# A hybrid decoder block on one core: the final norm's small operations over four token tiles at once, and the A products of two heads issued by turns

## The chip, the cores and the metric

The kernel runs on one core of a Trainium2 chip, as one program. The metric is the device time of one execution in microseconds, taken as the median of a few executions. The core's engines are TensorE (PE in the profile, with its weight loads as PEld), VectorE (DVE), ScalarE (ACT), GpSimd (POOL) and SyncE (SP), which issues the DMAs of this kernel. Each engine takes its own instructions in the order in which they stand in the program.

## The reference

```python
h = rmsnorm(x, norm_g) * (1 + scale) + shift          # scale, shift, gate from silu(c) @ ada_w + ada_b
p = h @ w_in                                          # (2048, 1024) @ (1024, 9344)
c_val, c_gate, c_og, ts, r_og, g_conv, g_rwkv = split(p)
# A: GLU, causal depthwise convolution of width 31, layer norm, swish, SiLU gate
y_conv = (silu(layernorm(conv31(c_val * sigmoid(c_gate)))) * silu(c_og)) @ w_conv_out
# B: RWKV-7, 16 heads of 64, delta-rule state, one step per token
state = state * w_t - (state @ kk_t) * b_t + v_t * k_t
o_t = state @ r_t
y_rwkv = ((groupnorm(o) + sum(r * k * r_k) * v) * silu(r_og)) @ w_rwkv_out
m = sigmoid(g_conv) * y_conv + sigmoid(g_rwkv) * y_rwkv
x = x + gate * (m @ w_out)
return x * rsqrt(mean(x * x) + 1e-6) * final_g        # the final norm
```

Everything is float32, batch 1, 2048 tokens, 1024 channels, one layer.

## The kernel before

The tokens are worked in four blocks of 512 (`TB`), each of four token tiles of 128 (`NTT`). A float32 product is split into three products of rounded high and low parts (`mm3k`, line 206: high by high, high by low, low by high), which is most of what PE does.

The first part of the kernel goes through the blocks, and in each through four groups of four heads (two pairs of two heads). For a pair, `pair` (lines 457 to 573) makes the decay factors, the keys, receptances and values by the input projection, and from them two tiles: `KR` (keys and receptances) and `BK` (the other side of each product). The **A products** (line 534) are then, for each chunk of 64 tokens, the products of `BK` with `KR` inside one head. One head fills 64 of the 128 partitions, so a product uses half of the array's rows: head 0 (`hh` = 0) the first 64, head 1 the others. The 8 chunks of a block go in two halves of four (`c4`); in each half every head has one PSUM tile of tag `aux` (`pA[hh]`), of which there are three (`PAB`), also used by the other small products of a pair. DVE masks each finished tile into `As` (line 537), which frees the tile. Then a correction of some of its rows (line 543), and for the whole group: small blocks of `As` go by DMA through DRAM to `La` (lines 611 to 616), POOL inverts triangles in 31 steps (lines 625 and 627), the result comes back by DMA, DVE transposes (line 653), and PE multiplies (lines 657 and 666). After that runs the recurrence over the 8 chunks: PE products of lines 684, 689 and 695, each followed by a small DVE operation (lines 686, 691, 699). Between all these PE works on projections (line 206) for gates and for the convolution (line 774, 30 DVE operations per channel tile).

The second part (from line 983) goes through the blocks again: `rproj` (line 986) and `cproj` (line 973) project the two branches into `mr` tiles, with two PSUM tiles `main` that line 993 and line 979 empty on DVE; then the output projection in four column pieces (`part`, lines 1090 to 1092). `addx` (line 1095) adds the residual on DVE and lets ACT sum squares into `sq4`, one column per token tile and piece. **`finish`** (line 1102) ends a token tile: it sums the four columns (line 1105), scales and adds (1106), takes the inverse root by `rsqrt` (lines 126 to 131: one starting guess and three rounds of three operations), scales the two halves of the tile (line 1111) and issues their output DMAs (line 1113). For blocks 0 to 2 the four token tiles are finished after the whole block, and the next block's `rproj` follows; in the last block each token tile is finished as soon as it is done.

The instructions of each engine are put in order by a scheduler when the program is built. It sees dependences, free buffers and priorities; the order of the source decides only where it has a choice.

Of the kernel before, what the change touches and what calls it, by code (L numbers as in the profile page):

```python
# [9 lines left out]
F32 = mybir.dt.float32  # L10
# [3 lines left out]
ALU = mybir.AluOpType  # L14
AX = mybir.AxisListType
# [3 lines left out]
P = 128  # L19
D = 1024  # L20
KT = D // P
TB = 512
NTT = TB // P
# [58 lines left out]
def hybrid_block(ctx: ExitStack, tc: tile.TileContext, x, vecs, convk, w2a2, final_g, ada, w_in, w_co, w_ro, w_o, crow, out,  # L82
                 seq=2048, groups=(0, 1, 2, 3), phase2=True, dbg=None):
    nc = tc.nc
# [38 lines left out]
    def rsqrt(y, x_, pool, eng, t=None):  # L123
        if t is None:
            t = pool.tile(list(x_.shape), F32, name="rs_t", tag="rs_t")
        eng.tensor_scalar(out=y.bitcast(I32), in0=x_.bitcast(I32), scalar1=-0.5, scalar2=float(0x5F3759DF),
                          op0=ALU.mult, op1=ALU.add)
        for _ in range(3):
            eng.tensor_tensor(out=t, in0=y, in1=y, op=ALU.mult)
            eng.scalar_tensor_tensor(out=t, in0=t, scalar=-0.5, in1=x_, op0=ALU.mult, op1=ALU.mult)  # L130
            eng.scalar_tensor_tensor(out=y, in0=t, scalar=1.5, in1=y, op0=ALU.add, op1=ALU.mult)
# [324 lines left out]
    def pair(b, q_, pr, h, lora, uv, Asb, rn, res):  # L456
# [30 lines left out]
        KR = l3.tile([P, NCH // 2, 4 * CH], F32, name="KR", tag="KR", bufs=KRB)  # L487
# [38 lines left out]

        for c4 in range(NCH // 4):
            pA = [pa.tile([P, 2, 256], F32, name="aux", tag="aux") for _ in range(2)]
            for c in range(4):
                cc, e = (c4 * 4 + c) // 2, c % 2  # L530
                es = slice(e * 128, e * 128 + 128)
                for hh in range(2):
                    hs = slice(64 * hh, 64 * hh + 64)
                    nc.tensor.matmul(pA[hh][:, c // 2, es], BK[hs, cc, es], KR[hs, cc, es],  # L534
                                     start=(c == 0), stop=(c == 3), skip_group_check=True)
            for hh in range(2):
                nc.vector.tensor_tensor(  # L537
                    out=Asb[:, hh, c4 * 4:c4 * 4 + 4, :].rearrange("p (a e) n -> p a (e n)", e=2),
                    in0=pA[hh], in1=flat(maskA).unsqueeze(1).broadcast_to([P, 2, 256]), op=ALU.mult)
# [521 lines left out]
    for b in range(NB):  # L1061
# [16 lines left out]
        for cb in range(4):  # L1078
# [20 lines left out]
                sq = f2.tile([P, 256], F32, name="fsq", tag="fsq", bufs=1)  # L1099
                nc.scalar.activation(sq, xt, AF.Square, accum_out=sq4[:, t0, cb:cb + 1])  # L1100

            def finish(tt):
                t0 = b * TB + tt * P
                vs = f2.tile([P, 1], F32, name="vs", tag="vs")
                nc.vector.tensor_reduce(out=vs, in_=sq4[:, tt, :], axis=AX.X, op=ALU.add)
                nc.vector.tensor_scalar(out=vs, in0=vs, scalar1=1.0 / D, scalar2=RMS_EPS, op0=ALU.mult, op1=ALU.add)
                rs = f2.tile([P, 1], F32, name="rs2", tag="rs2")
                rsqrt(rs, vs, f2, nc.vector)
                for half in range(2):
                    hs = slice(half * 512, half * 512 + 512)  # L1110
                    nc.vector.scalar_tensor_tensor(out=xts[tt][half], in0=xts[tt][half], scalar=rs, in1=fg[:, hs],
                                                   op0=ALU.mult, op1=ALU.mult)
                    nc.sync.dma_start(out[t0:t0 + P, hs], xts[tt][half])

            ws = []
            for kh in range(2):
# [4 lines left out]
            if end:  # L1121
                for tt in range(NTT):
                    for kh in range(2):
                        part(tt, kh, *ws[kh])
                    addx(tt)
                    finish(tt)
            else:
                for tt in range(NTT):
                    addx(tt)
        if b + 1 < NB:  # L1130
            for tt in range(NTT):
                finish(tt)
        if b + 1 < NB:
            mr = mnew()
            rproj(b + 1, ohl, mr)
# [34 lines left out]
```

## Time and profile before

| | |
|---|---|
| median of 3 runs | 3034.74 us (3031.83 to 3035.33) |
| the profiled execution | 3047.45 us, its span 3045.7 us |
| PE busy | 2914.9 us, 96% of the span |
| DVE busy | 2058.4 us, 68% |
| POOL busy | 1250.1 us, 41% |
| ACT busy | 935.2 us, 31% |
| granted TensorE clock, mean | 0.975 |
| DMA moved | 699.24 MB, the queue's packets 68.0% of 16 engines' time |

The profile is of one execution. Busy time counts every instruction from its start to its modelled end, and matmuls overlap, so PE's work is better read from the distance of one start to the next. The first operation of line 993, in the second part, starts at 2467.2 us. A source line can stand for many instructions: line 206 has 15552, the A products 1024 records, two for each of 512 instructions, since a float32 product is done in two passes.

### The profile page before, as it was taken

What the parts mean: (1) busy time and instruction counts of PE and PEld (TensorE: products, weight loads), DVE (VectorE), ACT (ScalarE), POOL (GpSimd) and SP (SyncE); (2) the same over time, 40 slices, a digit from 0 to 9 for tenths busy, and PEclk for the clock granted to TensorE, in tenths of its full rate; (3) what the DMA queues carried; (4) which work ended last, traced back from release to release, by engine and by line L of the source; (5) the groups of instructions that cost most, each with busy time, mean ns of one, the idle gap of its engine ahead of it and who ended that gap; (6) DMA issues with size and microseconds to landing.
All of it is one profiled execution on the core that took longest, in us unless ns stands there. A gap on an engine that the chain in (4) does not pass through costs nothing.

```text
span 3045.7 us, 64763 instructions
## 1 busy us (share of the span) xinstructions
PE 2914.9 (96%) x25672; PEld 2735.9 (90%) x25672; DVE 2058.4 (68%) x3896; ACT 935.2 (31%) x1759; POOL 1250.1 (41%) x1786
## 2 busy tenths in 40 slices
PE   6999998999999999899999999999999999899998
PEld 6889998989989899899999999999999988788988
DVE  6587877686867676668676767676779635776433
ACT  4433434332323232233232323232323222333201
POOL 3455555434343425143434263625467204565000
PEclk9899999999999999999999999999999999999999
DMA  8666758564758578847474777655647778889674
GB/s 303 205 234 209 251 196 282 199 235 145 250 185 260 187 242 287 235 137 246 151 246 139 246 254 252 199 185 165 212 141 246 229 264 309 320 311 344 239 280 163
DMA packets 368673, 699.24 MB, mean 230 GB/s; under 512 B 136241, under 2 KB 154993, under 8 KB 368370
## 3 DMA queue, kind: packets, MB, share of 16 engines
q1 hardware_dynamic: 368370, 695.10, 68.0%
q8 instruction: 202, 3.31, 0.4%
q14 instruction: 101, 0.83, 0.1%
HBM read 506.14 MB, written 187.70 MB: 228 GB/s over the span
## 4 chain that ended last, share of the span: by engine, by line
PE 61%; DMA 16%; DVE 9%; POOL 7%; SPq 3%; issue 2%; ACT 2%; ACTq 0%; DVEq 0%; POOLq 0%
PE ps_main L206 43%; DMA w_st<-w_in_t 3%; PE aux L534 2%; POOL TT L627 2%; POOL itmp L625 2%; DMA w_st<-w_ro_t 2%; DMA w_st<-w_co_t 2%; PE pout L1091 2%; PE pout L1092 2%; PE pout L1090 2%; PE xo L689 2%; DVE acc L774 1%; DMA w_gr<-grow_d 1%; PE xo L684 1%; PE xo L695 1%
## 5 line engine op out<-in xcount | busy, mean ns | idle before, releaser
L206 PE MATMUL ps_main<-h_hi,w_hi 128*128 128x256 f32 x4608 | 971.3, 289 | 12.2 <-ACT w_hi L189 3.4
L206 PE MATMUL ps_main<-h_hi,w_lo 128*128 128x256 f32 x4608 | 965.4, 289 | 8.5 <-POOL w_lo L191 5.0
L206 PE MATMUL ps_main<-h_lo,w_hi 128*128 128x256 f32 x4608 | 971.3, 289 | 0.0
L206 PEld LDWEIGHTS ps_main<-h_hi,w_hi 128*128 128x128 f32 x4608 | 735.3, 194 | 24.1 <-ACT w_hi L189 3.9
L206 PEld LDWEIGHTS ps_main<-h_hi,w_lo 128*128 128x128 f32 x4608 | 731.8, 194 | 17.5 <-POOL w_lo L191 6.3
L206 PEld LDWEIGHTS ps_main<-h_lo,w_hi 128*128 128x128 f32 x4608 | 733.9, 194 | 8.1 <-issue 0.5
L774 DVE SCALAR_TENSOR_TENSOR acc<-u,ck,acc 128x512 f32<-128x512 f32 x928 | 698.6, 753 | 20.8
L625 POOL TENSOR_TENSOR itmp<-La,TT 128x126 f32<-128x126 f32 (+22 forms) x496 | 180.2, 363 | 140.9 <-DMA La<-dA 106.1
L627 POOL TENSOR_TENSOR TT<-TT,itmp 128x126 f32<-128x126 f32 (+22 forms) x496 | 188.2, 379 | 37.3
L681 ACT ACTIVATE Se<-S,pe 128x128 f32<-128x128 f32 x256 | 89.0, 395 | 239.4 <-DVE S L699 239.2
L191 POOL TENSOR_TENSOR w_lo<-w_st,w_hi 128x1024 fp32r<-128x1024 f32 x47 | 113.6, 2417 | 112.8 <-ACT w_hi L189 106.2
L699 DVE TENSOR_TENSOR S<-xo,Se 64x128 f32<-64x128 f32 x256 | 73.5, 287 | 104.1 <-PE xo L695 100.8
L189 ACT CAST w_hi<-w_st 128x1024 fp32r<-128x1024 f32 x71 | 74.2, 1046 | 182.4 <-DMA w_st<-w_in_t 147.4
L534 PE MATMUL aux<-KR,BK 64*128 64x128 f32 x1024 | 121.5, 307 | 7.4 <-POOL BK L517 4.1
L534 PEld LDWEIGHTS aux<-KR,BK 64*128 64x128 f32 x1024 | 104.2, 208 | 18.7 <-POOL BK L517 4.3
L562 POOL TENSOR_TENSOR BK<-BK,pe 128x1024 f32<-128x1024 f32 x32 | 62.0, 1939 | 140.7 <-PE aux L534 113.1
L691 DVE TENSOR_TENSOR uv<-xo,rn 64x256 f32<-64x256 f32 x128 | 53.8, 420 | 90.7 <-PE xo L689 88.8
L686 DVE TENSOR_TENSOR XO<-xo,XO 128x256 f32<-128x256 f32 x128 | 53.7, 420 | 89.9 <-PE xo L684 70.5
L537 DVE TENSOR_TENSOR As<-aux,maskA 128x512 f32<-128x512 f32 x128 | 83.8, 685 | 36.9 <-PE aux L534 35.6
L684 PE MATMUL xo<-S,KR 128*128 128x128 f32 x512 | 83.0, 285 | 15.0 <-DVE S L699 14.9
L786 ACT ACTIVATE th<-ps_main 128x512 f32<-128x512 f32 x64 | 38.1, 596 | 190.1 <-PE ps_main L206 168.9
L431 ACT ACTIVATE t<-ps_main,mu 128x512 f32<-128x512 f32 x96 | 65.6, 683 | 97.4 <-PE ps_main L206 90.4
(301 smaller groups left out, 5318.2 us busy)
## 6 DMA issues: line engine op xcount, KB each, us to landing
w_hi<-kh_in SPq DMA_DIRECT2D x219, 512.0 KB, 5.1
w_lo<-kl_in SPq DMA_DIRECT2D x219, 512.0 KB, 4.0
w_st<-w_in_t SPq DMA_DIRECT2D x73, 512.0 KB, 4.9
kh_in<-w_hi SPq DMA_DIRECT2D x71, 512.0 KB, 2.9
kl_in<-w_lo SPq DMA_DIRECT2D x71, 512.0 KB, 3.7
w_hi<-kh_ro SPq DMA_DIRECT2D x32, 512.0 KB, 5.6
w_lo<-kl_ro SPq DMA_DIRECT2D x32, 512.0 KB, 5.5
w_hi<-kh_co SPq DMA_DIRECT2D x32, 512.0 KB, 5.5
```

Source lines behind the costliest of these rows:

```text
L189: nc.scalar.copy(hi, st)
L191: lo_eng.tensor_tensor(out=lo, in0=st, in1=hi.bitcast(F32), op=ALU.subtract)
L206: nc.tensor.matmul(ps[:, qs], ww[:, k, :], aa[k][:, qs], start=(k == 0 and t == 0 and q == 0), stop=(k == KT - 1 and t == 2 and q == ms - ...
L431: nc.scalar.activation(t1, ps, AF.Identity, scale=mu1[:, mi:mi + 1])
L534: nc.tensor.matmul(pA[hh][:, c // 2, es], BK[hs, cc, es], KR[hs, cc, es], start=(c == 0), stop=(c == 3), skip_group_check=True)
L537: nc.vector.tensor_tensor(out=Asb[:, hh, c4 * 4:c4 * 4 + 4, :].rearrange("p (a e) n -> p a (e n)", e=2), in0=pA[hh], in1=flat(maskA).unsqu ...
L625: nc.gpsimd.tensor_tensor(out=tmp[:, :ni, :nt], in0=La[:, j:j + 1, j + 1:].broadcast_to([P, ni, nt]), in1=TT[:, :ni, j:j + 1].broadcast_to ...
L627: nc.gpsimd.tensor_tensor(out=TT[:, :ni, j + 1:], in0=TT[:, :ni, j + 1:], in1=tmp[:, :ni, :nt], op=ALU.add)
L681: nc.scalar.mul(Se[:, q, :], Sg[:, q, :], R[q]["pe"][:, c:c + 1])
L684: nc.tensor.matmul(xo[:, q, :], R[q]["KR"][:, cc, es], Sg[:, q, :], start=(q == 0), stop=(q == 1), skip_group_check=True)
L699: nc.vector.tensor_tensor(out=Sg[hs, :, hs], in0=xo[hs, 2:4, hs], in1=Se[hs, :, hs], op=ALU.add)
L774: nc.vector.scalar_tensor_tensor(out=acc if i + 1 < HALO else yj, in0=u[:, i:i + TB], scalar=ck[:, j, i:i + 1], in1=acc, op0=ALU.mult, op1 ...
```

## The change

Two places of the source change.

In `pair`, the eight A products of a half were traced chunk by chunk with the heads inside, and the scheduler could pull one head's four products together. Now the first product of head 0 comes first, the first product of head 1 is tied behind it, and the other six, chunk by chunk with the heads inside, are tied behind that one (`issue_after` adds a dependence of order alone on the same engine).

In the second part, `finish` takes a list of token tiles. Blocks 0 to 2 call it once with all four: the sum, the scaling, and the ten operations of `rsqrt` work on 128x4 instead of 128x1, and the eight scalings and output DMAs follow. The last block calls it as before, for one tile at a time.

```diff
         for c4 in range(NCH // 4):
             pA = [pa.tile([P, 2, 256], F32, name="aux", tag="aux") for _ in range(2)]
-            for c in range(4):
+            def aprod(c, hh):
                 cc, e = (c4 * 4 + c) // 2, c % 2
                 es = slice(e * 128, e * 128 + 128)
-                for hh in range(2):
-                    hs = slice(64 * hh, 64 * hh + 64)
-                    nc.tensor.matmul(pA[hh][:, c // 2, es], BK[hs, cc, es], KR[hs, cc, es],
-                                     start=(c == 0), stop=(c == 3), skip_group_check=True)
+                hs = slice(64 * hh, 64 * hh + 64)
+                return nc.tensor.matmul(pA[hh][:, c // 2, es], BK[hs, cc, es], KR[hs, cc, es],
+                                        start=(c == 0), stop=(c == 3), skip_group_check=True)
+            with tc.issue_after(aprod(0, 0).ins):
+                second = aprod(0, 1)
+            with tc.issue_after(second.ins):
+                for c in range(1, 4):
+                    for hh in range(2):
+                        aprod(c, hh)
...
-            def finish(tt):
-                t0 = b * TB + tt * P
-                vs = f2.tile([P, 1], F32, name="vs", tag="vs")
-                nc.vector.tensor_reduce(out=vs, in_=sq4[:, tt, :], axis=AX.X, op=ALU.add)
+            def finish(tts):
+                n = len(tts)
+                vs = f2.tile([P, NTT], F32, name="vs", tag="vs")[:, :n]
+                nc.vector.tensor_reduce(out=vs, in_=sq4[:, tts[0]:tts[0] + n, :], axis=AX.X, op=ALU.add)
                 nc.vector.tensor_scalar(out=vs, in0=vs, scalar1=1.0 / D, scalar2=RMS_EPS, op0=ALU.mult, op1=ALU.add)
-                rs = f2.tile([P, 1], F32, name="rs2", tag="rs2")
-                rsqrt(rs, vs, f2, nc.vector)
-                for half in range(2):
-                    ...
+                rs = f2.tile([P, NTT], F32, name="rs2", tag="rs2")[:, :n]
+                rsqrt(rs, vs, None, nc.vector, f2.tile([P, NTT], F32, name="rs_t", tag="rs_t")[:, :n])
+                for i, tt in enumerate(tts):
+                    t0 = b * TB + tt * P
+                    for half in range(2):
+                        hs = slice(half * 512, half * 512 + 512)
+                        nc.vector.scalar_tensor_tensor(out=xts[tt][half], in0=xts[tt][half], scalar=rs[:, i:i + 1],
+                                                       in1=fg[:, hs], op0=ALU.mult, op1=ALU.mult)
+                        nc.sync.dma_start(out[t0:t0 + P, hs], xts[tt][half])
...
-                    finish(tt)
+                    finish((tt,))
...
-            for tt in range(NTT):
-                finish(tt)
+            finish(range(NTT))
```

Since a scheduler sets the order, nearly every stretch of every engine's order moves a little. Three places show what is meant. In the rows that follow, a row is an instruction (or several equal ones), with what it writes and reads; line numbers after the change are larger by 7 from the old line 541 on, and by up to 9 in `finish`.

**PE, the second half of a pair in the third block.** `aux_22009` is head 0's tile and `aux_22010` head 1's; `KR_21827` and `BK_21828` are the pair's tiles, `late_20716` belongs to the group before. Before:

```order
L534 MATMUL aux_21998<-KR_21827,BK_21828 128x128
L534 MATMUL aux_22009<-KR_21827,BK_21828 128x128 x4
L206 MATMUL ps_main_22028<-h_hi_16065,w_hi_22024 128x256 x2
L206 MATMUL ps_main_22028<-h_lo_16066,w_hi_22024 128x256 x2
L206 MATMUL ps_main_22028<-h_hi_16065,w_lo_22025 128x256 x2
L206 MATMUL ps_main_22028<-h_hi_16071,w_hi_22024 128x256 x2
L666 MATMUL late_20716<-As_19992,Qs_20715 32x32 x16
L666 MATMUL late_20716<-As_19993,Qs_20715 32x32 x16
L534 MATMUL aux_22010<-KR_21827,BK_21828 128x128 x4
L206 MATMUL ps_main_22028<-h_lo_16072,w_hi_22024 128x256 x2
```

After, the end of the first half with what follows it, and, seven rows of line 206 later, the rest:

```order
L534 MATMUL aux_21998<-KR_21827,BK_21828 128x128
L534 MATMUL aux_22009<-KR_21827,BK_21828 128x128
L206 MATMUL ps_main_22028<-h_hi_16065,w_hi_22024 128x256 x2
L206 MATMUL ps_main_22028<-h_lo_16066,w_hi_22024 128x256 x2
L206 MATMUL ps_main_22028<-h_hi_16065,w_lo_22025 128x256 x2
```

In the continuation the tile of head 0 and that of head 1 take turns:

```order
L673 MATMUL late_20716<-As_19992,Qs_20715 32x32 x16
L673 MATMUL late_20716<-As_19993,Qs_20715 32x32 x16
L534 MATMUL aux_22010<-KR_21827,BK_21828 128x128
L534 MATMUL aux_22009<-KR_21827,BK_21828 128x128
L534 MATMUL aux_22010<-KR_21827,BK_21828 128x128
L534 MATMUL aux_22009<-KR_21827,BK_21828 128x128
L534 MATMUL aux_22010<-KR_21827,BK_21828 128x128
L534 MATMUL aux_22009<-KR_21827,BK_21828 128x128
L534 MATMUL aux_22010<-KR_21827,BK_21828 128x128
L206 MATMUL ps_main_22120<-h_lo_16030,w_hi_22116 128x256 x2
```

Before, four products of head 0 stood together, and later four of head 1. Now one product of head 0 stands alone, and the other seven stand by turns. Over the whole program the 512 products stood in 83 unbroken runs, with 231 products that had no neighbour of the other head in their run; now they stand in 93 runs, with 10 such products.

**DVE, the end of block 0 in the second part.** `xt` are the residual tiles, `rs` the inverse roots, `mr` the tiles of `rproj`, `o_lo` an operand of the next block. Before, the second pair of token tiles begins:

```order
L1111 SCALAR_TENSOR_TENSOR xt_31892<-xt_31892,rs_32399,fg 128x512
L1111 SCALAR_TENSOR_TENSOR xt_31894<-xt_31894,rs_32399,fg 128x512
L1106 TENSOR_SCALAR vs<-vs 128x1 x2
L943 TENSOR_TENSOR o_lo_33025<-ot,o_hi_33026 128x512
L993 SCALAR_TENSOR_TENSOR mr_32453<-rth,ps_main 128x512
L943 TENSOR_TENSOR o_lo_33023<-ot,o_hi_33024 128x512
L126 TENSOR_SCALAR rs_32418<-vs 128x1
L126 TENSOR_SCALAR rs_32437<-vs 128x1
L129 TENSOR_TENSOR rs_t<-rs_32418 128x1
L129 TENSOR_TENSOR rs_t<-rs_32437 128x1
```

After, the same stretch, from the first `mr` to the second:

```order
L1000 SCALAR_TENSOR_TENSOR mr_32408<-rth,ps_main 128x512
L131 SCALAR_TENSOR_TENSOR rs_32380<-rs_t,rs_32380 128x4
L1120 SCALAR_TENSOR_TENSOR xt_31888<-xt_31888,rs_32380,fg 128x512
L1120 SCALAR_TENSOR_TENSOR xt_31890<-xt_31890,rs_32380,fg 128x512
L1120 SCALAR_TENSOR_TENSOR xt_31892<-xt_31892,rs_32380,fg 128x512
L1120 SCALAR_TENSOR_TENSOR xt_31894<-xt_31894,rs_32380,fg 128x512
L1120 SCALAR_TENSOR_TENSOR xt_31896<-xt_31896,rs_32380,fg 128x512
L1120 SCALAR_TENSOR_TENSOR xt_31898<-xt_31898,rs_32380,fg 128x512
L1120 SCALAR_TENSOR_TENSOR xt_31900<-xt_31900,rs_32380,fg 128x512
L1120 SCALAR_TENSOR_TENSOR xt_31902<-xt_31902,rs_32380,fg 128x512
L950 TENSOR_TENSOR o_lo_32976<-ot,o_hi_32977 128x512
L1000 SCALAR_TENSOR_TENSOR mr_32409<-rth,ps_main 128x512
```

Before, two chains of small operations (two token tiles side by side in each) and four scalings stood on either side of the first `mr`. Now there is one chain ahead of it, and all eight scalings stand between the first and the second.

**SP, the output DMAs of block 0.** The `w_hi` and `w_lo` rows load weights of `rproj` for PE, `rth` its gates. Before, the second four outputs:

```order
L1113 DMA out<-xt_31896 128x512
L183 DMA w_lo<-kl_ro_10384 128x1024
L1113 DMA out<-xt_31898 128x512
L1113 DMA out<-xt_31900 128x512
L182 DMA w_hi<-kh_ro_10403 128x1024
L1113 DMA out<-xt_31902 128x512
L1074 DMA xt_33282<-x_in 128x512
L990 DMA rth<-gr_d_3_270 128x512
```

After, the last five of all eight:

```order
L1122 DMA out<-xt_31894 128x512
L962 DMA bt<-bv_d_5_120 128x512
L1122 DMA out<-xt_31896 128x512
L1122 DMA out<-xt_31898 128x512
L1122 DMA out<-xt_31900 128x512
L183 DMA w_lo<-kl_ro_10384 128x1024
L1122 DMA out<-xt_31902 128x512
L182 DMA w_hi<-kh_ro_10403 128x1024
L997 DMA rth<-gr_d_3_270 128x512
```

The outputs stand closer together, and the same weight loads stand behind seven or eight of them in one stretch instead of behind two groups.

4 lines of the change are left out of this document (removed).

## The prediction

> **What bounds the kernel now.** I read the page's head and chain first, then PE's busy time by stretches.
>
> ```profile
> span 3045.7 us, 64763 instructions
> ...
> PE 2914.9 (96%) x25672; PEld 2735.9 (90%) x25672; DVE 2058.4 (68%) x3896; ACT 935.2 (31%) x1759; POOL 1250.1 (41%) x1786
> ...
> PE 61%; DMA 16%; DVE 9%; POOL 7%; SPq 3%; issue 2%; ACT 2%; ACTq 0%; DVEq 0%; POOLq 0%
> ```
>
> ```profile
> 100.00:600.00 500.00, 474.33 (x4388) 0.95 0.66 224
> ...
> 1700.00:2300.00 600.00, 593.00 (x5848) 0.98 0.63 205
> ...
> 2500.00:2700.00 200.00, 185.12 (x1033) 0.97 0.90 326
> 2700.00:2900.00 200.00, 199.53 (x1239) 1.00 0.79 280
> ```
>
> The second fence has a stretch in a row: its length, PE's busy time, its granted clock, the DMA share and GB/s. PE is busy for 96% of the span and holds 61% of the chain. Between 1700 and 2300 us it idles for 7 of 600 us. So PE time that is taken away should shorten the program nearly one for one, except where PE waits already: 26 us of 500 in the first block, and 15 us of 200 around the end of block 0 in the second part. In the first of these a gain can be lost. In the second lies the other half of the change.
>
> **The A products.** What they cost hangs on which head stands beside which. PE's timeline in the first block, records of one line merged (a product is two records):
>
> ```profile
> 402.18 2.05 PE L534 MATMUL aux<-KR,BK 64*128 64x128 f32 x24
> 404.16 0.50 PE L206 MATMUL ps_main<-h_lo,w_hi 128*128 128x256 f32 x2
> ...
> 406.02 0.40 PE L206 MATMUL ps_main<-h_lo,w_hi 128*128 128x256 f32 x2
> 406.26 0.28 PE L206 MATMUL ps_main<-h_hi,w_lo 128*128 128x256 f32 x1
> 406.47 1.16 PE L534 MATMUL aux<-KR,BK 64*128 64x128 f32 x8
> 407.55 0.39 PE L206 MATMUL ps_main<-h_hi,w_lo 128*128 128x256 f32 x1
> ```
>
> ```profile
> 560.85 1.82 PE L534 MATMUL aux<-KR,BK 64*128 64x128 f32 x22
> 562.61 0.71 PE L695 MATMUL xo<-uv,tk 128*128 128x128 f32 x4
> 563.25 0.48 PE L534 MATMUL aux<-KR,BK 64*128 64x128 f32 x2
> 563.66 0.50 PE L206 MATMUL ps_main<-h_hi,w_lo 128*128 128x256 f32 x2
> ```
>
> A run costs the distance from its start to the next start. The run of 24 (eight products by turns, then four of head 0) takes 404.16 - 402.18 = 1.98 us, that of 22 (by turns, then three of head 0) 562.61 - 560.85 = 1.76, that of 2 takes 0.41, that of 8 (four of head 1) 1.08. From these:
> - One product beside its own head: 1.98 - 1.76 = 0.22 us.
> - Entering and leaving a run: 0.41 - 0.22 = 0.19 behind the first start, and in front of it 406.47 - 406.26 = 0.21 where a record of line 206 takes 0.12 (two in 0.24), so 0.09 more: 0.28 us in all.
> - Eight by turns: 1.98 - 0.19 - 4 x 0.22 = 0.91, so 0.114 us each. Two heads use the array's two halves at the same time.
>
> By the order of the built program, 231 of the 512 products have no neighbour of the other head, 281 have one, in 83 runs; after the change 10, 502 and 93. Before: 83 x 0.28 + 281 x 0.114 + 231 x 0.22 = 106.1 us. After: 26.0 + 57.2 + 2.2 = 85.4 us. **PE's work falls by 20.7 us.** The ten more runs are in it, at 2.8 us.
>
> The row for entering and leaving is the place for a rule. The Trainium skill, "TensorEngine Tiling (Array Packing)", Key Properties, says that a change of tiling mode drains TensorE, which speaks against a change that makes ten more runs. If each of their 20 switches cost a whole product's 0.27 us, they would cost 5.4 us and the saving would be 18.1; the run of 2 with its 0.19 us measures less, so I keep 20.7.
>
> What hides part of it? PE waits for the chain of a group (A products, mask, inversion, transposes) in few places:
>
> ```profile
> PE late L657 <- DVE T L653: 4.0, 3, 3.4
> ...
> PE xo L684 <- DVE S L699: 14.9, 12, 2.4
> PE xo L695 <- DVE uv L691: 12.0, 12, 2.8
> ```
>
> ```profile
> L653 DVE STREAM_TRANSPOSE T<-As x8: 256/296/304, 1236.4 to 1240.2; 32x128 f32<-32x128 f32 x8
> ...
> L657 PE MATMUL late<-T,As x64: 191/191/212, 1279.0 to 1280.0; 32*32 32x32 f32 x64
> ```
>
> ```profile
> L537 DVE TENSOR_TENSOR As<-aux,maskA 128x512 f32<-128x512 f32 x128 | 83.8, 685 | 36.9 <-PE aux L534 35.6
> ```
>
> In a typical group the transposes start last at 1240.2 us and PE takes them up at 1279.0: 38 us of cover. Only three times, for 4.0 us together, does PE wait there. In such a group the saved PE time (20.7/16 = 1.3 us) is only cover that is gone, so 3 x 1.3 = 3.9 us are not gained. The change also lets head 0's last mask wait until all products of the half are done, so one mask more (0.685 us) stands at the end of each pair; where the chain is exposed that costs 3 x 0.7 = 2.1 us, elsewhere the 38 us hide it. Left: 20.7 - 3.9 - 2.1 = **14.7 us**. Bounds: all of it, 21; and nothing, if the first block (9 of the 33 halves that had a head by itself) and others turn it into waits.
>
> **The final norm.** Where block 0 ends, PE waits for DVE twice:
>
> ```profile
> PE ps_main L206 <- DVE mr L993: 11.8, 4, 5.5
> ```
>
> ```profile
> 2616.43 0.39 PE L206 MATMUL ps_main<-m_hi,w_lo 128*128 128x512 f32 x1
> 2620.44 0.51 PE L206 MATMUL ps_main<-m_hi,w_hi 128*128 128x512 f32 x1 [3.62 <-DVE mr L993]
> ...
> 2633.43 0.79 PE L206 MATMUL ps_main<-m_hi,w_hi 128*128 128x512 f32 x1 [5.55 <-DVE mr L993]
> ...
> 2638.28 0.43 PE L206 MATMUL ps_main<-m_hi,w_lo 128*128 128x512 f32 x1
> ```
>
> ```profile
> 2612.28 5.83 DVE L1111 SCALAR_TENSOR_TENSOR xt<-xt,rs,fg 128x512 f32<-128x512 f32 x4
> ...
> 2619.71 0.68 DVE L993 SCALAR_TENSOR_TENSOR mr<-rth,ps_main 128x512 f32<-128x512 f32 x1
> ...
> 2621.57 1.13 DVE L129 TENSOR_TENSOR rs_t<-rs 128x1 f32<-128x1 f32 x2
> 2622.66 1.27 DVE L130 SCALAR_TENSOR_TENSOR rs_t<-rs_t,vs 128x1 f32<-128x1 f32 x2
> ...
> 2629.43 2.74 DVE L1111 SCALAR_TENSOR_TENSOR xt<-xt,rs,fg 128x512 f32<-128x512 f32 x4
> 2632.69 0.68 DVE L993 SCALAR_TENSOR_TENSOR mr<-rth,ps_main 128x512 f32<-128x512 f32 x1
> ```
>
> ```profile
> L129 DVE TENSOR_TENSOR rs_t<-rs x48: 142/156/1259, 2605.8 to 3040.5; 128x1 f32<-128x1 f32 x48
> L1111 DVE SCALAR_TENSOR_TENSOR xt<-xt,rs,fg x32: 737/747/1783, 2612.3 to 3041.8; 128x512 f32<-128x512 f32 x32
> ```
>
> PE can run two groups (5.6 us each: 24 products at 0.234) ahead of `mr`, then it needs a PSUM tile back. DVE has the second pair's chain and scalings in the way from 2621.57 to 2632.1. PE loses 3.62 + 5.55 = 9.2 us, and then runs the next products at 0.43 us instead of 0.23 (from 2633.43 to 2638.28, 11 distances, 4.85 us for 2.6), about 2 us more for each wait: 13 us.
>
> The change takes 36 small operations a block away, 108 in all. Wherever they are not in PE's way this is worth nothing. Here the second chain goes (2621.57 to 2629.43, 7.9 us of the wait), but all eight scalings now stand between the first `mr` and the second. Uncrowded, 8 x 0.6 us (start to start) plus `mr` and a split of 1.2 are 6 us against PE's 5.6: hardly a wait. Slowed as in 2612.28 (5.74 us for four) they are 11.5 + 1.9 = 13.4, a wait of 8 us. I take the middle, 4 us with 2 us of slow products: 13 - 6 = 7, less 1 for the later first `mr`, **6 us gained**, between 13 gained and 3 lost. SP's queue holds weight loads behind the outputs for one long stretch now, where before it had two; a tag of seven weight buffers lies between, and PE waited for such a load nowhere in this stretch. The ends of blocks 1 and 2 lost 2.6 us (11.8 - 9.2), and I leave them alone; the last block's tail is unchanged.
>
> **The sum.** 3047.45 us, the profiled execution's own time (1.75 over its span), less 14.7, less 6: 3026.7. The median of the runs shown is 12.7 us lower, so on that footing 3034.7 - 20.7 = **3014 us**. The scheduler also reorders everything else. The waits of the recurrence above (lines 684 and 695, 27 us in 24 places) can grow or shrink by a third, 9 us either way; I take nothing.
>
> **The rivals.**
> - *The chain takes the PE time back.* For it: 26 us idle in the first block, and chain waits in the later ones; against it: 7 us idle of 600 later, and 38 us of cover. Then only the norm's 6 us are left, or half of them: 3029 to 3034 us, within 0.2% or on its edge. Chance 0.13.
> - *The scalings are blocked.* A scaling took up to 1.78 us and a small operation up to 1.26 us, when they lay beside POOL's work. If all nine operations with two inputs and all eight scalings of block 0 are slowed, DVE needs 11 us ahead of the first `mr` and 14 between it and the second: PE loses some 2 + 10 us and 4 at the slow clock, 16 instead of 13. Time: 3034.7 - 14.7 + 3 = 3023 us. Chance 0.15, inside the forecast of "faster". The Trainium skill, "SBUF — State Buffer", SBUF: two separate sides, gives a reason: a VectorE operation with two SBUF inputs and a GpSimd operation that reads SBUF exclude each other for a whole instruction. The rows above fit it, since of two equal small operations one took about 1.1 us and the pair 1.13; it would hold for one chain as for two.
> - *PE waits for the freed tile.* Slower. The lone first product is held by nothing, but the other seven need the tile that the first half's mask frees, and PE runs in order. If DVE takes one operation of line 774 first, PE stands for that and the mask: 0.753 + 0.685 = 1.4 us.
>
> ```profile
> L774 DVE SCALAR_TENSOR_TENSOR acc<-u,ck,acc 128x512 f32<-128x512 f32 x928 | 698.6, 753 | 20.8
> ```
>
> From 19 of the 32 pairs on it eats all 26.7 us (20.7 and 6); in 30 pairs the time is 3034.7 + 42 - 26.7 = 3050. Against it: the run of head 1 needed the same tile before, stood 2.3 us behind (404.16 to 406.47), and PE's waits name no mask. Chance 0.07.
>
> **How the numbers follow.** The likeliest case is 3014. Its terms' bounds, 6 up and 15 down for the products, 7 and 9 for the norm, 9 for the rest, give about 14 below and 17 above when they don't all meet: 3000 to 3031, which takes in the second rival and the near end of the first. About 0.2%, 6 us, is what a measurement of this kernel can tell from no change. Faster than 3028.7: 0.80. Within: 0.13. Slower than 3040.8: 0.07.
>
> **What would show it.** Line 534's records should come in by-turn runs, with the sum of their distances down by 20 us. PE's busy share between 1700 and 2300 us should stay at 98% or more; if it falls to 95%, the first rival holds. The wait of PE for `mr` (11.8 us) should fall below 8; if there is one wait of 8 us or more in block 0, the scalings were blocked. A wait of line 534 for line 537, in total over 20 us, would make the forecast wrong, as would a growth of the waits of lines 684 to 695 by 20 us.

## The result, and the profile after

The changed kernel takes 3045.80 us (median of 9 executions, 3036.50 to 3055.94), the kernel before 3035.06 us (9, 3022.09 to 3038.25). The ratio is 1.004, with a 95% interval of 1.0027 to 1.0053: **slower by 11 us**. A second comparison (e11) gave 1.0036 (1.0018 to 1.0053). The prediction was 3014 us, faster by 20.7.

The page of the changed kernel begins like this; columns as before.

```profile
span 3045.7 us, 64668 instructions
...
PE 2881.0 (95%) x25672; PEld 2701.5 (89%) x25672; DVE 2054.3 (67%) x3788; ACT 936.6 (31%) x1759; POOL 1256.3 (41%) x1786
```

Both profiled executions have a span of 3045.7 us, so the two profiles side by side don't show the 11 us: that of before was 12 us above its kernel's median, that of after within 2 us of its own. What they do show is PE: busy for 2881.0 us instead of 2914.9 in the same span. It has less work, and 34 us more in which it waits. The group of the A products says where the work went (busy time and mean duration, then the idle time before it). Before:

```profile
L534 PE MATMUL aux<-KR,BK 64*128 64x128 f32 x1024 | 121.5, 307 | 7.4 <-POOL BK L517 4.1
```

After:

```profile
L534 PE MATMUL aux<-KR,BK 64*128 64x128 f32 x1024 | 92.1, 297 | 2.6 <-POOL KR L522 1.1
```

The group fell by 29.4 us, and as much came back as waits. PE's waits after the change (total, times, longest), those that grew, with one of the recurrence for comparison:

```profile
PE ps_main L206 <- DVE mr L1000: 15.6, 2, 9.2
PE ps_main L206 <- DMA w_lo<-kl_in: 15.4, 2, 14.5
PE xo L702 <- DVE uv L698: 11.3, 10, 2.9
...
PE late L746 <- POOL XO L741: 9.0, 5, 2.7
PE ps_main L206 <- POOL w_lo L191: 8.0, 7, 1.8
PE aux L557 <- DVE vv L435: 6.5, 4, 2.5
PE aux L575 <- POOL BK L569: 6.1, 5, 3.2
```

Two stand out. One is new: a single wait of 14.5 us for a weight load, which ends at 1244 us. The same line of the kernel before was 3.5 us in three. The other is the wait for `mr`, 11.8 us before: now two waits, at the ends of block 0 and block 1. PE's busy time by stretches (rows as in the prediction):

```profile
1700.00:2300.00 600.00, 584.03 (x5814) 555.86 (x5813) 435.27 (x791) 183.56 (x336) 297.85 (x447) 0.99 0.62 200
2500.00:2700.00 200.00, 181.74 (x1018) 152.44 (x1017) 120.18 (x182) 56.27 (x109) 109.78 (x76) 0.97 0.89 322
2700.00:2900.00 200.00, 192.31 (x1200) 171.06 (x1199) 110.92 (x183) 63.97 (x136) 56.90 (x39) 0.98 0.74 264
```

Idle grew by 9 us in the first of these stretches, by 3 at the end of block 0 and by 7 at the end of block 1. The work in a stretch is not quite the same before and after: the first `mr` of the second part starts at 2453.0 us instead of 2467.2. With equal spans, the profile after is thus 14 us ahead there, and loses this lead in the second part. DVE at the end of block 0, in the order of time (start, duration, operation, count):

```profile
2606.09 0.68 DVE L1000 SCALAR_TENSOR_TENSOR mr<-rth,ps_main 128x512 f32<-128x512 f32 x1
2606.69 0.73 DVE L131 SCALAR_TENSOR_TENSOR rs<-rs_t,rs 128x4 f32<-128x4 f32 x1
2607.45 13.56 DVE L1120 SCALAR_TENSOR_TENSOR xt<-xt,rs,fg 128x512 f32<-128x512 f32 x8
2620.94 1.75 DVE L950 TENSOR_TENSOR o_lo<-ot,o_hi 128x512 fp32r<-128x512 f32 x1
2622.61 0.67 DVE L1000 SCALAR_TENSOR_TENSOR mr<-rth,ps_main 128x512 f32<-128x512 f32 x1
```

And POOL in the same microseconds:

```profile
2607.36 13.11 POOL L1062 TENSOR_TENSOR y<-y,rl 128x512 f32<-128x512 f32 x8
```

The eight scalings took 1.7 us each beside eight products of POOL, and the second `mr` came 16.5 us after the first. PE's row there (behind the bracket, the wait and who ended it):

```profile
2623.34 0.79 PE L206 MATMUL ps_main<-m_hi,w_hi 128*128 128x512 f32 x1 [9.23 <-DVE mr L1000]
```

### The profile page after: what moved, and what is told of

It is laid out like the page before. It is cut to its first block, busy times and chain, and to the rows that moved or that the text cites. A ratio compares the mean times of both kernels' runs of the same rounds, so it can differ in the third digit from the quotient of the medians.

```text
span 3045.7 us, 64668 instructions
## 1 busy us (share of the span) xinstructions
PE 2881.0 (95%) x25672; PEld 2701.5 (89%) x25672; DVE 2054.3 (67%) x3788; ACT 936.6 (31%) x1759; POOL 1256.3 (41%) x1786
## 4 chain that ended last, share of the span: by engine, by line
PE 37%; DMA 9%; DVE 7%; POOL 5%; issue 3%; SPq 1%; ACT 1%; POOLq 0%; DVEq 0%; ACTq 0%
PE ps_main L206 28%; DMA w_gr<-grow_d 1%; POOL TT L634 1%; POOL itmp L632 1%; PE pout L1097 1%; PE pout L1099 1%; PE pout L1098 1%; PE xo L696 1%; DMA w_lo<-kl_in 1%; PE xo L691 1%; PE aux L534 1%; PE xo L702 1%; DVE xt L1120 1%; DMA w_st<-w_co_t 1%; DMA La<-dA 1%
## 5 line engine op out<-in xcount | busy, mean ns | idle before, releaser
L793 ACT ACTIVATE th<-ps_main 128x512 f32<-128x512 f32 x64 | 38.2, 597 | 206.7 <-PE ps_main L206 178.5
L696 PE MATMUL xo<-XO,As 64*64 64x64 f32 x1024 | 89.8, 226 | 5.7 <-DVE XO L693 5.7
L534 PE MATMUL aux<-KR,BK 64*128 64x128 f32 x1024 | 92.1, 297 | 2.6 <-POOL KR L522 1.1
L696 PEld LDWEIGHTS xo<-XO,As 64*64 64x64 f32 x1024 | 70.4, 135 | 26.5 <-DVE XO L693 7.4
L761 ACT ACTIVATE th<-ps_main 128x512 f32<-128x512 f32 x64 | 38.1, 595 | 179.2 <-PE ps_main L206 134.2
```

The source lines that it names most:

```text
L534: return nc.tensor.matmul(pA[hh][:, c // 2, es], BK[hs, cc, es], KR[hs, cc, es], start=(c == 0), stop=(c == 3), skip_group_check=True)
L696: nc.tensor.matmul(xo[pr_, q, hs], As[q][pr_, hh, c, kcol(e)], XO[pr_, c, q, hs], start=(q == 0 and hh == 0), stop=(q == 1 and hh == 1), s ...
```

## The experiments

All ratios are to the kernel before on the same chip, with 95% intervals. The first theory was that the by-turns products do shorten the program and the batched norm takes it back; the rival, that the products' gain is lost in the first part. Both turned out incomplete.

| kernel | ratio | interval |
|---|---|---|
| changed kernel | 1.0040, again 1.0036 | 1.0027 to 1.0053, 1.0018 to 1.0053 |
| e1 by-turns products alone | 1.0012 | 0.9999 to 1.0025 |
| e2 batched norm alone | 1.0012 | 0.9997 to 1.0028 |
| e3 products head by head | 1.0004 | 0.9989 to 1.0019 |
| e4 by turns, two batches of two | 1.0005 | 0.9989 to 1.0022 |
| e5 changed, `y<-y,rl` on DVE | 1.0032 | 1.0018 to 1.0047 |
| e6 changed, gate's loads earlier | 1.0005 | 0.9991 to 1.0019 |
| e7 changed, both edits | 1.0001 | 0.9985 to 1.0016 |
| e8 before, both edits | 0.9989 | 0.9972 to 1.0006 |
| e9 before, one row | 1.0059 | 1.0040 to 1.0079 |
| e10 changed, one row | 1.0154 | 1.0129 to 1.0179 |
| e12 before, norm traced later | 1.0014 | 0.9999 to 1.0030 |
| e13 by turns, gate earlier | 0.9973 | 0.9962 to 0.9984 |
| e14 by turns, two batches, gate earlier | **0.9967** | 0.9956 to 0.9979 |
| e15 by turns alone, one row | 1.0139 | 1.0121 to 1.0157 |
| e16 before, gate earlier | 0.9997 | 0.9983 to 1.0010 |
| e17 changed, gate's write in larger pieces | 1.0013 | 0.9998 to 1.0028 |
| e18 two batches, gate's write from ScalarE | 1.0002 | 0.9987 to 1.0017 |

### The change taken apart (e1, e2, e4)

e1 and e2 each hold one of the two places of the diff. e4 is the changed kernel with

```diff
-            finish(range(NTT))
+            finish((0, 1))
+            finish((2, 3))
```

> The kernel before with the A products by turns as in the changed kernel (same 93 runs, 502 products by turns, 10 alone), and the final norm one token tile at a time as before. Theory 'norm' (the by-turns products do shorten the program, the batched norm takes it back and 11 us more): 10 to 20 us faster than before, about 3015 to 3025 us, and PE's wait for mr in the second part stays at 8 to 12 us. Rival 'first part' (the products' gain turns into other waits, and the new order costs by itself): 3035 to 3046 us, with the lead of the first part gone before the first mr.

> The kernel before with only the final norm's small operations over four token tiles (blocks 0 to 2); A products as before (83 runs, 281 by turns, 231 alone). Theory 'norm': 10 to 25 us slower than before, 3045 to 3060 us, PE's wait for mr at the ends of blocks 0 and 1 together 15 us or more. Rival 'first part': within 5 us of before, 3030 to 3040 us.

> The changed kernel with the final norm of blocks 0 to 2 in two batches of two token tiles instead of one of four: 54 small operations fewer than before instead of 108, and four scalings instead of eight in a row. Theory 'norm', if it is the row of eight scalings that holds the second mr: 10 to 20 us faster than the changed kernel, 3025 to 3035 us, no single wait for mr of 8 us or more. Rival 'first part': within 5 us of the changed kernel, 3040 to 3050 us.

The by-turns products alone gained nothing that can be seen: 3042.65 us against 3038.83. PE's waits in e1:

```profile
PE ps_main L206 <- DMA w_lo<-kl_in: 16.9, 2, 15.4
PE ps_main L206 <- DVE mr L1000: 14.4, 2, 12.3
```

So the long wait for a weight load belongs to the products' order, not to the norm, and the waits for `mr` came to almost as much with the norm per token tile: the first theory falls. At the end of block 0 the wait was even longer than in the changed kernel, 12.3 us against 9.2. There the second `mr` came 18.2 us after the first, behind the small operations and scalings of the other token tiles:

```profile
2609.91 0.67 DVE L1000 SCALAR_TENSOR_TENSOR mr<-rth,ps_main 128x512 f32<-128x512 f32 x1
...
2628.07 0.67 DVE L1000 SCALAR_TENSOR_TENSOR mr<-rth,ps_main 128x512 f32<-128x512 f32 x1
```

```profile
2628.80 0.79 PE L206 MATMUL ps_main<-m_hi,w_hi 128*128 128x512 f32 x1 [12.30 <-DVE mr L1000]
```

The rival is not right either: e1's profile has the span of the kernel before, 3045.7 us, and starts its first `mr` at 2454.7 us, so it too is 12.5 us ahead there and loses that in the second part.

The batch has a price all the same: the changed kernel is 0.0024 to 0.0028 above e1 and 0.0031 to 0.0035 above e4, 7 to 11 us (each about 6 uncertain). What it consists of is seen only in part. From the first `mr` to the end the profiles take 578.5 us before, 591.0 in e1, 592.7 in the changed kernel (592.7 again in e11) and 583.9 in e4. With the batch of four the wait at the end of block 0 was shorter than in e1, and one was added at the end of block 1, where e1 has none for `mr`; all eight scalings stand ahead of the first `mr` there (DVE, then PE):

```profile
2762.73 8.44 DVE L1120 SCALAR_TENSOR_TENSOR xt<-xt,rs,fg 128x512 f32<-128x512 f32 x8
```

```profile
2771.83 0.79 PE L206 MATMUL ps_main<-o_hi,w_hi 128*128 128x512 f32 x1 [6.34 <-DVE mr L1000]
```

In sum the waits for `mr` are 15.6 us (14.1 in e11) against 14.4 in e1, so they alone don't make the price, and the rest of it stays open. Two batches of two cost nothing that can be seen against e1, though in e4 one wait stayed above the 8 us that was expected at most:

```profile
PE ps_main L206 <- DVE mr L1000: 10.6, 3, 8.7
```

In the old order the batch (e2) was not separated from no change; its wait for `mr` was 11.5 us, as before.

### What PE's work is worth, and what the order costs (e3, e9, e10, e11, e15)

e3 ties four products of head 0 ahead of four of head 1, to add work.

> The kernel before with the A products of a half tied head by head (four of head 0, then four of head 1): 85 runs, 122 products by turns, 390 alone, by the costs of the prediction 124.8 us of PE work instead of 106.1, 18 us more; norm as before. It asks what PE work of these products is worth at the end of the program, without moving much of the order. If PE's time counts one for one: 18 us slower, 3053 us. If waits of the chain hide it: 0 to 6 us slower, 3035 to 3041 us. The theory 'norm' expects 12 to 20 us slower, 'first part' 0 to 6.

It was no lever: the group took 124.4 us instead of 121.5, 3 us more where 18 were worked out, and the time was the same. It shows one thing beside: on PE 14988 of the 25672 instructions stand at another place than before (16748 in e1), so a new order as such need not cost anything. The next runs change the work without moving an instruction: head 1's products read head 0's rows, in the old order, the changed kernel's, and that of e1. Head 1's own products are left out.

```diff
-                hs = slice(64 * hh, 64 * hh + 64)
+                hs = slice(0, 64)
```

> The kernel before, every instruction of every engine in the same place, but the A products of head 1 read the rows of head 0 (so head 1's A is left out and head 0's stands twice). No product then runs beside another: by the prediction's costs 83 x 0.28 + 512 x 0.22 = 135.9 us instead of 106.1, 30 us more PE work. Theory 'PE work counts' (a product's time reaches the end, and it is the changed order that costs): 20 to 30 us slower than before, ratio 1.007 to 1.010. Theory 'other engines and transfers set the pace' (PE only waits less where it works more): 0 to 10 us slower, ratio 1.000 to 1.003.

> The changed kernel, every instruction in the same place, with the same edit: head 1's A products read the rows of head 0, so head 1's A is left out. 93 x 0.28 + 512 x 0.22 = 138.7 us instead of 85.4, 53 us more PE work. Theory 'PE work counts': 40 to 53 us slower than the changed kernel, and 15 to 25 us slower than the kernel before with this edit, which does the same PE work in the old order: the price of the new order. Theory 'other engines and transfers set the pace': 0 to 25 us slower than the changed kernel, most of it once its waits of some 38 us are used up, and about as fast as the kernel before with this edit.

> A products alone in the new order (norm one token tile at a time), every instruction in the same place as in that kernel, but all products read head 0's rows, so head 1's A is left out: 138.7 us of work for them by the prediction's costs. At equal work the old order took 3057 us and the changed kernel's 3085. If the 28 us lie in the order that the A products force, 3077 to 3085 us (ratio 1.0125 to 1.015); if they lie in the batched norm, 3057 to 3065 us (1.006 to 1.0085); by halves, 3068 to 3074 us.

> The changed kernel itself, on the chip of these runs, as the footing for the run with one row, and a second profile. Ratio 1.002 to 1.005. If the waits found in its first profile belong to the order, they come again: w_lo<-kl_in 13 to 16 us in one wait, mr 14 to 17 us, and A products at 88 to 93 us between starts. If they were chance, they differ by half.

The group in e9:

```profile
L534 PE MATMUL aux<-KR,BK 64*128 64x128 f32 x1024 | 142.6, 289 | 2.6 <-POOL KR L522 2.2
```

In e10:

```profile
L534 PE MATMUL aux<-KR,BK 64*128 64x128 f32 x1024 | 141.7, 285 | 2.3 <-POOL KR L522 1.4
```

The work is now equal, and the times are not: 3057.01 us in the old order, 3084.71 in the new, **28 us for the order alone**, that of the products and the batch together (ratios 1.0059 and 1.0154; the difference is 10 us uncertain). In e15 (141.2 us for the group) the ratio is 1.0139: 0.0080 above e9, so 24 us (8 uncertain) come with the products' order, and the rest, 0.0015 or 5 us (9 uncertain), with the batch. The profiles of e9 and e15, both at a granted clock of 0.980, differ by less than the medians, 11 us of span: e15 starts its first `mr` 1 us later (2469.0 against 2468.1) and takes 10 us more from there on. The same runs give the worth of PE's work where the order is held: 0.0059 or 18 us for 21.1 (e9 against before), 33 us for 49.6 (e10 against the changed kernel again, 3051.37), 0.0127 or 39 us for 50.0 (e15 against e1). Two thirds to six sevenths of it reach the end, each with several us of uncertainty. Part of these times goes with the clock: its mean was 0.9757 in e9 and 0.9752 in e10, 0.0021 below the kernels that they are held against, which by the figure of the last section is 4 us each; without these, e9 and e10 give 0.67 and 0.59. For the 29.4 us that the products saved, two thirds to six sevenths are 20 to 25 us, about what the prediction promised; the order took them back. The 121.5 us of the group before are the highest of the old order, and e2, e8, e12 and e16 have 115.0 to 117.8; by these the saving is 23 to 26 us, worth 15 to 22.

e11 shows that the waits are no chance: the wait for w_lo<-kl_in was 13.2 us with one of 12.2, and that for `mr` 14.1 us in two.

### The wait at the end of block 0 (e5, e7, e12)

e5 moves the eight products `y<-y,rl` off POOL (line 41: `OE, LE, CE = 0, 1, 1` instead of `0, 0, 1`); e12 traces the norm behind the next block's `rproj`.

> The changed kernel with the eight products y<-y,rl of the layer norm (line 1062) on DVE instead of POOL, 8 in each of blocks 1 to 3. In the profiles so far they run on POOL in one row of 11 to 13 us beside DVE's scalings and small operations, and DVE's second mr comes only behind that row. Theory 'POOL row' (that row, not the number of small operations, holds mr): PE's wait for mr falls from 15.6 us to under 6, the scalings take 0.6 to 0.8 us each, and the time is 8 to 14 us below the changed kernel's, about 3035 us (ratio to before 1.000). Rival 'number of operations in the way' (DVE has simply too much before mr, and gets 5 us more): mr wait 14 us or more, time not below the changed kernel's, ratio 1.004.

> The kernel before with the final norm of a block (per token tile, as before) traced behind the next block's rproj instead of ahead of it, so that DVE's mr operations stand ahead of the scalings and small operations. Theory 'DVE's norm in front of mr' (what mr waits for is the norm's work ahead of it): PE's wait for mr falls from 11.8 us to under 4, and the time by 5 to 12 us, ratio 0.996 to 0.998. Theory 'transfers set the pace there' (DMA engines are 88 to 93% busy from 2500 to 2800 us, and mr itself waits 20 us for rth<-gr_d): mr's wait for rth grows by as much, ratio 0.999 to 1.001.

e5's rival holds: the wait for `mr` rose to 20.7 us in four. With the gate's edit of the next section too (e7, whose ratio of 1.0001 lies between its two expectations), DVE shows why; the eight scalings are quick, but the eight products stand in front of `mr` themselves:

```profile
2596.98 0.68 DVE L1001 SCALAR_TENSOR_TENSOR mr<-rth,ps_main 128x512 f32<-128x512 f32 x1
2597.58 0.85 DVE L131 SCALAR_TENSOR_TENSOR rs<-rs_t,rs 128x4 f32<-128x4 f32 x1
2598.46 6.43 DVE L1121 SCALAR_TENSOR_TENSOR xt<-xt,rs,fg 128x512 f32<-128x512 f32 x8
2604.82 4.89 DVE L1063 TENSOR_TENSOR y<-y,rl 128x512 f32<-128x512 f32 x8
```

So POOL's row does double the scalings (13.56 us beside it, 6.43 without), and that is not enough: whatever stands between two `mr` operations counts. The Trainium skill, "SBUF — State Buffer", SBUF: two separate sides, gives a reason, an exclusive lock on the port that VectorE and GpSimd share, held for a whole instruction; the two rows agree with it. e12 gave no answer: the scheduler left four scalings on either side of the first `mr`, as before, and the wait was 12.1 us.

### The weight load (e6, e7, e8, e16, e17, e18)

SyncE's queue in the changed kernel, ahead of the long wait (start, length, line, DMA):

```profile
1229.02 0.43 SPq L645 DMA_DIRECT2D As<-dT  x1
1229.55 0.38 SPq L883 DMA_DIRECT2D grow_d<-hgate_col  x1
1229.97 0.58 SPq L764 DMA_DIRECT2D ro_d<-th  x1
1230.65 0.38 SPq L183 DMA_DIRECT2D w_lo<-kl_in  x1
```

PE took the load of 1230.65 up 13 us later:

```profile
1243.82 0.80 PE L206 MATMUL ps_main<-h_hi,w_lo 128*128 128x256 f32 x2 [14.55 <-DMA w_lo<-kl_in]
```

The median of such loads around this place (1195 to 1260 us) is 6.2 us from issue to landing:

```profile
w_lo<-kl_in SPq DMA_DIRECT2D x7, 512.0 KB, 6.2
```

`grow_d<-hgate_col` is the last step of the gate: its columns' sums, written once to DRAM at the end of the second block. In the old order five weight loads were issued between 1239.6 and 1243.6 us, ahead of the same write:

```profile
1239.63 0.38 SPq L183 DMA_DIRECT2D w_lo<-kl_in  x1
...
1243.23 0.59 SPq L183 DMA_DIRECT2D w_lo<-kl_in  x1
...
1250.34 0.37 SPq L876 DMA_DIRECT2D grow_d<-hgate_col  x1
```

In the new order the write stands ahead of the load that PE needs next. The wait cost some 2 us more than its own length: behind it PE's pairs of products started 0.43 us apart for 4.3 us, and 0.24 us apart after that. e6 reads the gate's last columns a group earlier, which moves the write too:

```diff
-                gate_cols(g)
+                for q in ((0,), (1, 2), (3,), ())[g]:
+                    gate_cols(q)
```

> The changed kernel with the last quarter of the gate's columns (gt<-ada_t, 4 loads) read one group earlier (two quarters at group 1 of block 1, the last at group 2, none at group 3), so that they don't stand with hf<-xT and the 16 As<-dT ahead of the weight load that PE waited 14.5 us for at about 1230 us. Theory 'queue' (that stall took a good part of the products' gain): the wait for w_lo<-kl_in falls from 15.4 to under 5 us and the time is 8 to 12 us below the changed kernel's, ratio 1.000 to 1.001. Rival 'PE's lead is lost anyway' (another wait takes its place): kl_in wait gone but time as the changed kernel's, ratio 1.003 to 1.005.

> The changed kernel with both edits: products y<-y,rl on DVE, and the gate's last loads a group earlier. Theory (the two stalls together took the gain): 16 to 25 us below the changed kernel, ratio to before 0.995 to 0.998. Rival (lost in many small waits elsewhere): ratio 1.002 or more.

> The kernel before with the same two edits (y<-y,rl on DVE, gate's last loads a group earlier). It sets what by-turns products and batched norm are worth once both stalls are out of the way: with the theory 'two stalls took the gain' this is 10 us or more slower than the changed kernel with both edits, at a ratio of 0.999 to 1.000; with the rival 'many small waits' the two are within 5 us of each other.

> The kernel before with the gate's last loads one group earlier and nothing else. PE waited there only 3.5 us for w_lo<-kl_in and 2.5 for w_hi<-kh_in, so theory 'the wait belongs to the new order': within 5 us of before, ratio 0.9985 to 1.000. Rival 'the edit helps any order by 10 us': ratio 0.997.

e6 takes the wait for the load to 4.9 us and the ratio to 1.0005, 10 us (6 uncertain) below the changed kernel. In the old order the same edit is worth nothing (e16, 0.9997). But it lets the scheduler move much else: 5273 of PE's instructions stand at another place. e7 and e8 are within 0.0012 of each other: with this one wait gone, and the batch of four still there, the products only break even. What in the gate's step held the load was still open, so e17 writes the same 4 KB in 128 pieces of 32 bytes instead of 1024 of 4 (which leaves the gate's columns in another order), and e18 gives the write to ScalarE's queue. Against the changed kernel and e4, they move nothing else but 8 and 4 of PE's instructions.

```diff
-            nc.sync.dma_start(grow_d.rearrange("(n p) -> p n", p=P), hgate_col)
+            nc.sync.dma_start(grow_d.rearrange("(p n) -> p n", p=P), hgate_col)
```

> The changed kernel with the write grow_d<-hgate_col laid out by partition: 128 pieces of 32 bytes instead of 1024 of 4 (so the gate's columns stand in another order in grow_d, and the gate is permuted); all other instructions stand where they stood but for a few products of line 206. Theory 'the small pieces of that write hold the weight load': landing of the write falls from 10.8 to under 4 us, the wait for w_lo<-kl_in from 13 to 15 us to under 6, the time by 8 to 12 us (ratio to before 1.000 to 1.001). Rival 'the gt, hf and As transfers ahead of it hold the load': wait 10 us or more, ratio 1.003 to 1.005.

> A products by turns, final norm in two batches, gate's loads where the changed kernel has them, but the write grow_d<-hgate_col issued by ScalarE instead of SyncE; the other instructions stand as in the run with two batches alone (ratio 1.0005). Theory 'small pieces', if another queue keeps them out of the weight load's way: wait for w_lo<-kl_in under 6 us, ratio 0.996 to 0.998. If the same 16 DMA engines are what the pieces hold, whoever issues them: wait 10 us or more, ratio 0.9995 to 1.0015. The rival (gt, hf, As) expects the latter too.

The changed kernel's transfers from 1231 to 1241 us (packets, MB and share of 16 engines), and in the window from 1229 that write's own row (size, us from issue to landing):

```profile
DMA packets 382, 0.54 MB, mean 54 GB/s; under 512 B 187, under 2 KB 187, under 8 KB 382
...
q1 hardware_dynamic: 382, 0.54, 87.1%
```

```profile
grow_d<-hgate_col SPq DMA_DIRECT2D x1, 4.0 KB, 10.8
```

In e17:

```profile
grow_d<-hgate_col SPq DMA_DIRECT2D x1, 4.0 KB, 1.6
```

```profile
PE ps_main L206 <- DMA w_lo<-kl_in: 5.3, 2, 4.7
```

In e18:

```profile
q10 hardware_dynamic: 1040, 0.00, 1.2%
...
grow_d<-hgate_col ACTq DMA_DIRECT2D x1, 4.0 KB, 10.8
```

```profile
PE ps_main L206 <- DMA w_lo<-kl_in: 12.7, 2, 11.7
```

While the small pieces were under way, 16 engines at 87% of their time moved 0.54 MB in 10 us. The pieces' own packets took little of that time, 1.2% of the engines' in e18; the packets of the other transfers were long, and these rows don't say why. In larger pieces the write landed in 1.6 us and the longest wait was 4.7 us; the ratio fell to 1.0013, 7 to 8 us (6 uncertain) where 8 to 12 were expected. From another queue the pieces held the load too, for 11.7 us of waiting. That part of e6 is shown: it is the write, not the `gt`, `hf` or `As` transfers. The Trainium skill, "DMA: Bandwidth & Descriptors", Rules for kernel authors, says that a transfer whose last dimension is not contiguous becomes one descriptor per element; 1040 packets for 1024 elements agree. Its section Issuing engines are not separate DMA queues says that transfers end on the same 16 engines whichever engine issued them; the 11.7 us of e18 agree.

### Put together (e13, e14)

> A products by turns, final norm one token tile at a time, and the gate's last loads one group earlier. Theory 'the order costs, and its largest piece is the wait for w_lo<-kl_in' (10 us by the changed kernel without and with the edit): 8 to 12 us below the by-turns products alone, ratio to before 0.997 to 0.999. Rival 'other waits take its place': ratio 1.000 to 1.002.

> A products by turns, final norm in two batches of two token tiles, and the gate's last loads one group earlier. Same theory, with the row of eight scalings broken up too: ratio to before 0.996 to 0.998, faster than either kernel. Rival: 1.000 to 1.002.

Both beat both kernels: 3022.63 and 3019.89 us against 3030.76 for the kernel before on that chip. Their mean granted clock was higher too, 0.981 against 0.978; by the figure of the last section 5 to 6 of their 8 and 11 us go with it, and whether the better order raised the clock is not shown. The page and the waits of e14:

```profile
PE 2875.1 (95%) x25672; PEld 2697.0 (89%) x25672; DVE 2055.4 (68%) x3824; ACT 935.5 (31%) x1759; POOL 1256.6 (42%) x1786
```

```profile
PE xo L702 <- DVE uv L698: 9.8, 11, 2.8
PE ps_main L206 <- DVE mr L1001: 9.7, 4, 4.9
PE aux L557 <- DVE vv L435: 8.4, 5, 3.3
PE ps_main L206 <- POOL w_lo L191: 7.6, 5, 1.8
...
PE aux L534 <- POOL KR L522: 5.3, 4, 2.4
...
PE ps_main L206 <- DMA w_lo<-kl_in: 3.3, 2, 3.0
```

The long wait for the load is gone and no wait for `mr` is above 5 us. What stays of the order's price are waits for `vv` (2.0 us before), `KR` (0.9) and the split weights (5.0): PE reaches these operations earlier than the engines that feed it. That reading was not tested on its own.

## Why the prediction was wrong

- **PE bounds the kernel, so its time shortens the program nearly one for one.** Near enough: with the order held, 0.67 to 0.87 of PE's work reached the end (0.59 at the least, with the clock's part taken off).
- **The A products, 20.7 us.** Too small: the group's busy time fell by 29.4. Counted as the prediction counts, from each start to the next without the waits, the profiles have 116.1 us before and 86.0 after. So the 85.4 worked out for the new order was right, and the 106.1 for the old one 10 us too low (4 to 6 by e2, e8, e12 and e16); its costs came from a few runs in two places of the first block. The rule on mode switches, with its 18.1, was further off.
- **What hides part, 3.9 and 2.1 us.** The waits that it named behaved: the transposes 5.6 us (4.0 before), the freed tile 0.4. The cover of 38 us held for the chain that it was measured on; the waits that grew lie elsewhere.
- **"I take nothing" for the rest, 9 us either way.** This is the step that failed. The term put at nothing measured 24 us (8 uncertain): that is what the scheduler's new order of the products costs at equal work. Some 7 to 10 of them are one wait, for a weight load behind a 4 KB write; the prediction had looked at SP's queue only at the end of block 0, while the new order moved it all through the first part. The cause of the rest stays open. The profiles show only where it is lost: of e1's lead of 12.5 us at the first `mr`, none is left at the end of a span as long as before.
- **The final norm, 6 us gained.** Wrong in sign: the batch of four cost 7 to 11 us in this order. The eight scalings of block 0 were slowed by POOL as the second rival said, with one wait of 9.23 us, and the prediction's own test of 8 us or more named it. But this is not what the batch cost, since e1, without the batch, waits 12.3 us there. What the batch added is at the end of block 1, which the prediction left alone: 15.6 - 9.2 = 6.4 us, against 2.6 in blocks 1 and 2 before. The rest of its price was not found.
- **The rivals.** The first was nearest, and its sign of 95% was half met (584 of 600 us, 97%): the PE time did come back as waits, though in other places than the chain, and with more on top. The third did not occur. None made the new order a cost of its own, and so the chance of slower, 0.07, was too small.

The sum, with what was measured: 20 to 25 us less from the products, 24 more from their order, 7 to 11 more from the batch; 6 to 15 us slower by these, 11 measured. This is no independent check, since the parts come from the same ratios, and each is 6 to 10 us uncertain.

## What to carry to other kernels

An edit under a scheduler is two edits, the work and the order, and they can be priced apart: change what an instruction reads so that its cost changes and its place does not, in both orders. Where PE is busy for 96%, a shorter stretch of its work is worth most of its length only if nothing late is waiting in the queues that feed it; look through these queues for slow small transfers before counting on it. In front of an operation that frees a tile for PE, count all that stands between two of them on that engine, and batch no further than the wait allows: here two tiles were as good as one, four were not.

## What the hardware showed beside

- A write of 4 KB in pieces of 4 bytes took 10.8 us to land, and a weight load issued behind it came late, from the same queue (PE waited 14.5 us) and from another (11.7); in pieces of 32 bytes the write took 1.6, and the wait was 4.7.
- Executions of one kernel differ in TensorE's mean granted clock, and the time follows: in 34 executions of the kernel before on one chip it lay between 0.973 and 0.981, and the time fell by 2.0 us for each 0.001 (correlation -0.78). That is most of the spread of 20 us, and the reason why one profile against one profile misleads here.
